# Six projections to the model width in a three-layer block: two matmuls of 256 columns become one of 512

## The chip, the core and the metric

The kernel runs on one core of one Trainium2 chip. The metric is device time in microseconds (us) of one launch. Before the change it was 1184.19, 1186.18 and 1185.54 us in three runs, median 1185.54 us.

## What is computed

The reference carries 256 tokens of width 1024 through three layers in float32: a Mamba-2 mixer with a convolutional feed-forward part ("ffn0"), differential attention with a second one ("ffn1"), and a layer with sparse attention beside a recurrent branch ("dsa") and a third one ("ffn2"). Each of the six parts ends in a projection back to the model width, whose result is added to `x`; the next part begins with a norm of that sum:

```python
for layer in range(DEPTH):
    ...
        mix = mamba2_mixer(x, ...)            # ... ends in  y @ out_w        2048 -> 1024
    ...
        mix = diff_attention(x, ...)          # ... ends in  o @ out_w        1024 -> 1024
    x = x + mix.astype(x.dtype)
    ff = conv_ffn(x, ...)                     # (silu(gate) * up) @ down_w    2816 -> 1024
    x = x + ff.astype(x.dtype)
```

The third layer has the same shape; its mixer ends in a 1024 to 1024 projection (`w_out_2`) whose result is scaled by a column of the modulation vector before it is added, as is that of its feed-forward part.

## The kernel before

**Two parts of every operand.** TensorE takes float32 operands here in a rounded form (`F32R`). To keep accuracy every operand is split into a high part (a rounded copy) and a low part (what is left). A product of W and x is three matmuls into the same PSUM tile: high by high, high by low, low by high. `mmB` (line 373) and `tileB_f` (line 780) write these three for each k tile of 128 rows, W stationary and x^T of 256 tokens moving, at lines 379 to 381 and 788 to 790.

**The weight stream.** Weights come from HBM in chunks through four `raw` buffers, SyncE issuing the DMA. `split` (line 242) makes of each piece (up to eight k tiles) `wh` on ScalarE (line 253) and `wl` on VectorE (line 257; at some steps on GpSimd, line 255). Both have five buffers, so pieces are split up to five ahead of TensorE, and a buffer comes free when TensorE has finished the piece that was in it.

**Steps.** The program is written as a list of steps, one for each piece. At the end of a step `step` (line 303) issues what was put off to it (the work behind a finished tile among that), then up to two splits, then a little background work. The engines' queues keep that order, apart from what the scheduler of the language puts forward.

**The projections.** `tileB` (line 421) makes one tile of 128 output channels: 22 k tiles for a feed-forward part (three pieces: 8, 8 and 6), 8 for `attn_out_w` and `w_out_2`. `tileB_f` does the same for the 16 k tiles of `ssm_out_w`. There are eight such tiles, m = 0 to 7, in each projection, and three PSUM buffers for them. When tile m is done, `add_x` (line 506) adds it to `x` on VectorE (line 509, or 511 with a scale), ScalarE squares the sum for the coming norm (line 440), and `mkraw` (line 393) makes unscaled high and low operands of the next part on ScalarE (line 396) and VectorE (line 397; two pairs where attention comes next). So the first tiles of the next part can begin before the norm is known; they need all eight tiles of `x`.

**The modulation.** From ffn0 to the end of ffn1 a vector product of 24 MB of weights runs beside all that, a little at each step (`ada`, line 546): a DMA of 256 KB into one of two buffers, and a multiply with a running sum on VectorE (line 553). During ffn0's and ffn1's projections and attention one such unit falls on each step.

Of the kernel before, what the change touches and what calls it, by code (L numbers as in the profile page):

```python
# [153 lines left out]
# columns of the constants  # L154
# [21 lines left out]
class Net:  # L176
# [3 lines left out]
    def __init__(self, ctx, tc, a, phases, dbg=None):  # L180
# [11 lines left out]
        self.whp = P("wh", self.NS)  # L192
        self.wlp = P("wl", self.NS)
# [35 lines left out]
    # -- weight stream --  # L229
# [12 lines left out]
    def split(self, pool=False):  # L242
# [8 lines left out]
        wh = self.whp.tile([128, 1024], F32R, name="wh")  # L251
        wl = self.wlp.tile([128, 1024], F32R, name="wl")
# [5 lines left out]
        self.spl[i] = (wh, wl)  # L258
# [13 lines left out]
    # -- ScalarE's function tables: one set at a time, changed where the program says --  # L272
# [75 lines left out]
    def pipe(self, n, stages, first=None):  # L348
        """item i runs its stage s at step i + s; of one step, `first` comes first, then later stages before earlier"""
# [14 lines left out]

    def ax(self):
        return self.axp.tile([128, 512], F32, name="ax")
# [5 lines left out]
    # -- W stationary, x^T moving: out [channels, tokens] --  # L372
    def mmB(self, out, src, kx, xh, xl, first, last, m=128):
        wh, wl = self.piece(src)
        n = len(kx)
        for a, k in enumerate(kx):
            h, l = wh[:, a * m:a * m + m], wl[:, a * m:a * m + m]
            nc = self.nc
            nc.tensor.matmul(out, h, xh[:, k, :], start=first and a == 0, stop=False)  # L379
            nc.tensor.matmul(out, h, xl[:, k, :], start=False, stop=False)  # L380
            nc.tensor.matmul(out, l, xh[:, k, :], start=False, stop=last and a == n - 1)  # L381

    def raw_tile(self):
        """unscaled operands [128, h/l, k, tokens and shift]"""
# [15 lines left out]
    def tileR(self, src, rw, shift, post, m=128, bg=1):  # L400
        """a tile from the operands before their scaling by token, which its result gets instead"""
# [3 lines left out]
        self.mmB(pt, src, range(8), rw[:, 0, :, 0:n], rw[:, 1, :, 0:n], True, True, m)  # L405
# [15 lines left out]
    def tileB(self, src, nk, xh, xl, post, m=128, bg=1, delay=1):  # L421
        pt = self.ps()[0:m, 0:T]
        k = 0
        while k < nk:
            n = min(8, nk - k)
            self.mmB(pt, src, range(k, k + n), xh, xl, k == 0, k + n == nk, m)
# [5 lines left out]
    # -- norms --  # L432
# [13 lines left out]
    def rstd_bc(self, parts, n, bcast=True):  # L446
        """1/sqrt(mean of squares + eps) of each token, on all partitions: [128, T] in PSUM"""
# [23 lines left out]
    def xn(self, i=0):  # L471
        h = self.xp.tile([128, 8, T], F32R, name=f"xh{i}")
        l = self.xp.tile([128, 8, T], F32R, name=f"xl{i}")
        return h, l

    def norm(self, g, shift=None):
        """the normed x, times the gains g(k), plus shift(k), in two parts"""
        nc = self.nc
        h, l = self.xn()
# [24 lines left out]
        return h, l  # L504
# [11 lines left out]
    def start_dsa(self):  # L516
        nc, P = self.nc, self.P
        # softplus(-lambda), times -8
# [12 lines left out]
    # -- c -> the six modulation vectors, a little at each step --  # L531
# [32 lines left out]
    # ---------------------------------------------------------------- Mamba-2  # L564
    def mamba(self, pool, nxt):
# [6 lines left out]
        xh, xl = self.norm(lambda k: P("ssm_ln_g", k))  # L572
# [74 lines left out]
        for t in range(8):  # L647
# [4 lines left out]
            else:  # L652
                self.tileB("ssm_in_w", 8, xh, xl, post)
        xs = self.xp.tile([128, 16, T], F32, name="rw")
        for t in range(16):
            self.tileB("ssm_in_w", 8, xh, xl, conv_post(t, xs[:, t, :]))
# [905 lines left out]
```

## Time and profile before

| What | Time |
|---|---|
| median of three runs | 1185.54 us |
| span of the profiled execution | 1186.9 us |
| TensorE busy in it | 1132.1 us |
| VectorE busy | 959.5 us |
| ScalarE busy | 712.5 us |
| GpSimd busy | 220.6 us |

The profiled execution is one launch; the span is from its first to its last instruction, and no other time of that launch is given. PE is TensorE's matmuls, PEld its weight loads, DVE VectorE, ACT ScalarE, POOL GpSimd, SP SyncE. A matmul's row gives a start and a duration; matmuls overlap, so what one costs in a stream is the distance between two starts, not the duration.

### The profile page before, as it was taken

Reading aid. Unit: us, or ns where it says so; the run is one execution under the profiler, and the core shown is the slowest. Engines: PE = TensorE matmul, PEld = TensorE weight load, DVE = VectorE, ACT = ScalarE, POOL = GpSimd, SP = SyncE. Lnnn points to the kernel's source line nnn. Section 1 sums busy time; section 2 is a strip of 40 time slices with the busy share of each in tenths; the row PEclk is TensorE's granted clock in tenths of the full one; section 3 lists DMA queues with packets and bytes.
Section 4 is the critical chain, followed back from the end, with each engine's and each line's share of the span. In section 5 each row is a group of like instructions: output and inputs, shape, how many; then the busy total and the mean of one; then the engine's idle time right before and its main releaser. Section 6 shows DMA issues by size and latency. Waiting matters only on the chain.

```text
span 1186.9 us, 23538 instructions
## 1 busy us (share of the span) xinstructions
PE 1132.1 (95%) x9174; PEld 1099.7 (93%) x9174; DVE 959.5 (81%) x1866; ACT 712.5 (60%) x1322; POOL 220.6 (19%) x180
## 2 busy tenths in 40 slices
PE   6899898999999989998899999899999999999997
PEld 5799897989999989988899999898999999999997
DVE  5897997789898888788899988768867888888752
ACT  6567665566666547876566664464587556666541
POOL 3203665242100114222320001100100023200010
PEclk9899999999999999999799999899999999999999
DMA  8455442647766886664366668844442653555440
GB/s 303 141 181 191 149 159 75 234 154 252 259 213 230 268 280 216 205 201 161 133 214 221 205 215 282 258 163 151 165 160 86 210 195 138 191 197 177 166 141 36
DMA packets 50190, 224.80 MB, mean 189 GB/s; under 512 B 5744, under 2 KB 10496, under 8 KB 31136
## 3 DMA queue, kind: packets, MB, share of 16 engines
q1 hardware_dynamic: 41616, 211.53, 52.1%
q10 hardware_dynamic: 7056, 7.46, 2.3%
q0 software_dynamic: 1408, 4.32, 1.2%
q8 instruction: 72, 1.18, 0.4%
q14 instruction: 38, 0.31, 0.1%
HBM read 222.11 MB, written 4.25 MB: 191 GB/s over the span
## 4 chain that ended last, share of the span: by engine, by line
PE 56%; DVE 16%; DMA 7%; issue 4%; ACT 3%; POOL 1%; POOLq 0%; ACTq 0%; DVEq 0%
PE mm L379 15%; PE mm L380 15%; PE mm L381 15%; DMA ada<-in_wada_dram 7%; DVE wl L257 4%; DVE ada L553 2%; DVE cv L817 2%; DVE ny L493 1%; PE mm L912 1%; PE mm L913 1%; PE mm L914 1%; PE mm L789 1%; ACT wh L253 1%; PE mm L788 1%; PE mm L790 1%
## 5 line engine op out<-in xcount | busy, mean ns | idle before, releaser
L253 ACT ACTIVATE wh<-raw 128x1024 fp32r<-128x1024 f32 (+2 forms) x360 | 369.6, 1030 | 267.4 <-PE mm L380 233.1
L257 DVE TENSOR_TENSOR wl<-raw,wh 128x1024 fp32r<-128x1024 f32 (+1 forms) x333 | 395.7, 1189 | 101.4 <-ACT wh L253 98.8
L379 PE MATMUL mm<-xh,wh 128*128 128x256 f32 x1624 | 466.9, 288 | 8.2 <-DVE cv L817 2.1
L380 PE MATMUL mm<-xl,wh 128*128 128x256 f32 x1624 | 461.4, 284 | 6.3 <-DVE xl L469 6.0
L381 PE MATMUL mm<-xh,wl 128*128 128x256 f32 x1624 | 459.8, 283 | 0.0
L379 PEld LDWEIGHTS mm<-xh,wh 128*128 128x128 f32 x1624 | 308.7, 190 | 17.4 <-issue 9.0
L380 PEld LDWEIGHTS mm<-xl,wh 128*128 128x128 f32 x1624 | 308.7, 190 | 8.4 <-DVE xl L469 8.0
L381 PEld LDWEIGHTS mm<-xh,wl 128*128 128x128 f32 x1624 | 308.7, 190 | 0.0
L444 POOL TENSOR_TENSOR sqacc<-sqacc,sq 128x256 f32<-128x256 f32 x42 | 49.3, 1174 | 563.2 <-ACT sq L440 561.7
L379 PE MATMUL mm<-hh,wh 128*128 128x256 f32 x528 | 147.4, 279 | 0.0
L381 PE MATMUL mm<-hh,wl 128*128 128x256 f32 x528 | 147.4, 279 | 0.0
L380 PE MATMUL mm<-hl,wh 128*128 128x256 f32 x528 | 147.4, 279 | 0.0
L817 DVE SCALAR_TENSOR_TENSOR cv<-mm,par,cv 128x255 f32<-128x255 f32 x240 | 114.3, 477 | 4.4 <-ACT cv L815 2.8
L379 PEld LDWEIGHTS mm<-hh,wh 128*128 128x128 f32 x528 | 99.2, 188 | 0.0
L380 PEld LDWEIGHTS mm<-hl,wh 128*128 128x128 f32 x528 | 99.2, 188 | 0.0
L381 PEld LDWEIGHTS mm<-hh,wl 128*128 128x128 f32 x528 | 99.2, 188 | 0.0
L255 POOL TENSOR_TENSOR wl<-raw,wh 128x1024 fp32r<-128x1024 f32 x27 | 71.9, 2668 | 132.3 <-ACT wh L253 132.2
L553 DVE SCALAR_TENSOR_TENSOR ada<-ada,silu_c 128x512 f32<-128x512 f32 x96 | 71.3, 744 | 21.8 <-DMA ada<-in_wada_dram 21.6
L815 ACT ACTIVATE cv<-mm,par 128x256 f32<-128x256 f32 x120 | 65.7, 548 | 0.3 <-PE mm L381 0.3
L379 PE MATMUL mm<-rw,wh 128*128 128x256 f32 (+2 forms) x168 | 51.1, 305 | 9.6 <-ACT wh L253 8.5
L380 PE MATMUL mm<-rw,wh 128*128 128x256 f32 (+2 forms) x168 | 51.9, 309 | 0.0
L440 ACT ACTIVATE sq<-x 128x256 f32<-128x256 f32 x49 | 20.0, 410 | 53.0 <-DVE x L509 34.2
(317 smaller groups left out, 1993.0 us busy)
## 6 DMA issues: line engine op xcount, KB each, us to landing
raw<-in_w_dram SPq DMA_DIRECT2D x148, 1024.0 KB, 4.9
ada<-in_wada_dram SPq DMA_DIRECT2D x96, 256.0 KB, 4.0
raw<-in_w_dram SPq DMA_DIRECT2D x23, 896.0 KB, 4.6
raw<-in_w_dram SPq DMA_DIRECT2D x6, 768.0 KB, 4.2
abc<-acs_scr ACTq DMA_DIRECT2D x16, 256.0 KB, 3.4
rel_bias_scr<-rel_bias_row POOLq DMA_DIRECT2D x8, 384.0 KB, 7.2
bias<-rel_bias_scr ACTq DMA_DIRECT2D x16, 128.0 KB, 4.4
x<-in_xT_dram SPq DMA_DIRECT2D x4, 256.0 KB, 4.1
```

The source lines that it names most:

```text
L253: nc.scalar.activation(wh[:, :n], src, AF.Copy)
L255: nc.gpsimd.tensor_tensor(wl[:, :n], src, wh[:, :n].bitcast(F32), op=ALU.subtract)
L257: self.pace = nc.vector.tensor_tensor(wl[:, :n], src, wh[:, :n].bitcast(F32), op=ALU.subtract)
L379: nc.tensor.matmul(out, h, xh[:, k, :], start=first and a == 0, stop=False)
L380: nc.tensor.matmul(out, h, xl[:, k, :], start=False, stop=False)
L381: nc.tensor.matmul(out, l, xh[:, k, :], start=False, stop=last and a == n - 1)
L440: nc.scalar.activation(s, self.x[:, k, :], AF.Square)
L444: nc.gpsimd.tensor_tensor(self.acc, self.acc, s, op=ALU.add)
L493: nc.vector.scalar_tensor_tensor(y, self.x[:, k, :], g(k), self.rsb, op0=ALU.mult, op1=ALU.mult)
L553: i = nc.vector.scalar_tensor_tensor(t, t, 1.0, self.sc[:, h * 512:h * 512 + 512], op0=ALU.mult, op1=ALU.mult, accum_out=self.part[:, h, m ...
L815: nc.scalar.activation(c, pt, AF.Identity, scale=w(2), bias=P(cb, ct))
L817: nc.vector.scalar_tensor_tensor(c[:, d:], pt[:, :T - d], w(2 - d), c[:, d:], op0=ALU.mult, op1=ALU.add)
```

## The change

In the six projections the two matmuls that share the weights' high part become one of 512 columns: it takes high and low part of x side by side, and leaves high by high in the first half of a PSUM bank and high by low in the second. Low by high still goes as 256 columns, onto the first half. On the way out `add_x` adds both halves to `x`, one after the other, so there are two VectorE instructions for each tile instead of one. The other matmuls stay as three. To let one access pattern reach both parts, pairs of tiles become one tile with a dimension of two (`wh`/`wl` to `ww`, `xh`/`xl` to `xx`, `hh`/`hl` to `hh`, and so on); sizes and numbers of buffers stay. Comments and docstrings go as well.

```diff
+    def ps_wide(self):
+        return self.ps().rearrange("p (a t) -> p a t", a=2)
...
-        wh = self.whp.tile([128, 1024], F32R, name="wh")
-        wl = self.wlp.tile([128, 1024], F32R, name="wl")
+        ww = self.wp.tile([128, 2, 1024], F32R, name="ww")
+        wh, wl = ww[:, 0], ww[:, 1]
...
+    def mm3(self, out, h, l, x, first, last):
+        nc = self.nc
+        if len(out.shape) == 3:
+            nc.tensor.matmul(out, h, x, start=first, stop=False)
+            nc.tensor.matmul(out[:, 0], l, x[:, 0], start=False, stop=last)
+            return
+        nc.tensor.matmul(out, h, x[:, 0], start=first, stop=False)
+        nc.tensor.matmul(out, h, x[:, 1], start=False, stop=False)
+        nc.tensor.matmul(out, l, x[:, 0], start=False, stop=last)
+
-    def mmB(self, out, src, kx, xh, xl, first, last, m=128):
-        wh, wl = self.piece(src)
+    def mmB(self, out, src, kx, xx, first, last, m=128):
+        ww = self.piece(src)
         n = len(kx)
         for a, k in enumerate(kx):
-            h, l = wh[:, a * m:a * m + m], wl[:, a * m:a * m + m]
-            nc = self.nc
-            nc.tensor.matmul(out, h, xh[:, k, :], start=first and a == 0, stop=False)
-            nc.tensor.matmul(out, h, xl[:, k, :], start=False, stop=False)
-            nc.tensor.matmul(out, l, xh[:, k, :], start=False, stop=last and a == n - 1)
+            c = slice(a * m, a * m + m)
+            self.mm3(out, ww[:, 0, c], ww[:, 1, c], xx[:, :, k, :], first and a == 0, last and a == n - 1)
...
-    def tileB(self, src, nk, xh, xl, post, m=128, bg=1, delay=1):
-        pt = self.ps()[0:m, 0:T]
+    def tileB(self, src, nk, xx, post, m=128, bg=1, delay=1, wide=False):
+        pt = self.ps_wide() if wide else self.ps()[0:m, 0:T]
...
     def add_x(self, m, pt, scale=None):
         nc = self.nc
-        if scale is None:
-            nc.vector.tensor_tensor(self.x[:, m, :], pt, self.x[:, m, :], op=ALU.add)
-        else:
-            nc.vector.scalar_tensor_tensor(self.x[:, m, :], pt, scale, self.x[:, m, :], op0=ALU.mult, op1=ALU.add)
+        for a in (1, 0):
+            if scale is None:
+                nc.vector.tensor_tensor(self.x[:, m, :], pt[:, a], self.x[:, m, :], op=ALU.add)
+            else:
+                nc.vector.scalar_tensor_tensor(self.x[:, m, :], pt[:, a], scale, self.x[:, m, :],
+                                               op0=ALU.mult, op1=ALU.add)
         self.square(m)
         self.mkraw(m)
...
         if pt is None:
-            pt = self.ps()[0:128, 0:T]
+            pt = self.ps_wide()
...
-            wh, wl = self.piece(src)
+            ww = self.piece(src)
             for a in range(n):
-                h, l = wh[:, a * 128:a * 128 + 128], wl[:, a * 128:a * 128 + 128]
-                nc.tensor.matmul(pt, h, fh(k + a), start=k + a == 0, stop=False)
-                nc.tensor.matmul(pt, h, fl(k + a), start=False, stop=False)
-                nc.tensor.matmul(pt, l, fh(k + a), start=False, stop=k + a == nk - 1)
+                c = slice(a * 128, a * 128 + 128)
+                self.mm3(pt, ww[:, 0, c], ww[:, 1, c], f(k + a), k + a == 0, k + a == nk - 1)
...
-        hh = pool.tile([128, NF, T], F32R, name="hh", bufs=1)
-        hl = pool.tile([128, NF, T], F32R, name="hl", bufs=1)
+        xx = self.norm(gs, shift=shift)
+        hh = pool.tile([128, 2, NF, T], F32R, name="hh", bufs=1)
...
-            self.tileB(down, NF, hh, hl, lambda pt, m=m: self.add_x(m, pt, scale and scale(m)))
+            self.tileB(down, NF, hh, lambda pt, m=m: self.add_x(m, pt, scale and scale(m)), wide=True)
...
-            self.tileB("attn_out_w", 8, oh, ol, lambda pt, m=m: self.add_x(m, pt))
+            self.tileB("attn_out_w", 8, oo, lambda pt, m=m: self.add_x(m, pt), wide=True)
...
-            self.tileB("w_out_2", 8, mh, ml, lambda pt, m=m: self.add_x(m, pt, self.mod[:, 16 + m:17 + m]))
+            self.tileB("w_out_2", 8, mx, lambda pt, m=m: self.add_x(m, pt, self.mod[:, 16 + m:17 + m]),
+                       wide=True)
```

## Rows read from the trace of the kernel before

**Rows 1.** The page: the span, and each engine's busy time, share and instructions.

```profile
span 1186.9 us, 23538 instructions
PE 1132.1 (95%) x9174; PEld 1099.7 (93%) x9174; DVE 959.5 (81%) x1866; ACT 712.5 (60%) x1322; POOL 220.6 (19%) x180
```

**Rows 2.** Windows, the six projections: stretch, length, busy times (instructions), clock, DMA.

```profile
206.00:234.70 28.70, 28.70 (x246) 28.70 (x245) 21.24 (x25) 15.60 (x24) 8.06 (x6) 1.00 0.64 210
368.00:429.70 61.70, 61.67 (x529) 61.47 (x527) 51.36 (x102) 32.82 (x48) 7.06 (x6) 1.00 0.79 268
541.00:561.60 20.60, 18.90 (x149) 18.29 (x148) 20.54 (x38) 13.15 (x22) 6.09 (x6) 0.97 0.66 215
697.60:759.30 61.70, 61.70 (x532) 61.70 (x530) 50.07 (x99) 31.54 (x43) 6.71 (x6) 1.00 0.81 265
957.60:981.00 23.40, 23.35 (x195) 23.14 (x194) 19.53 (x27) 13.98 (x25) 8.42 (x6) 1.00 0.58 208
1113.25:1174.90 61.65, 61.65 (x531) 61.65 (x530) 28.12 (x34) 23.26 (x31) 7.83 (x6) 1.00 0.30 103
```

**Rows 3.** Timeline, ends of tiles 0 and 7 in ffn0's projection, two engines.

```profile
375.49 0.28 PE L381 MATMUL mm<-hh,wl 128*128 128x256 f32 x1
376.44 0.42 DVE L509 TENSOR_TENSOR x<-mm,x 128x256 f32<-128x256 f32 x1
...
429.39 0.28 PE L381 MATMUL mm<-hh,wl 128*128 128x256 f32 x1
434.65 0.42 DVE L509 TENSOR_TENSOR x<-mm,x 128x256 f32<-128x256 f32 x1
435.63 0.61 PE L452 MATMUL ax<-onec,sq 128*128 128x1 f32 x4 [3.29 <-ACT sq L440]
```

**Rows 4.** Timeline, end of tile 7 in ffn1's and in ffn2's projection.

```profile
758.97 0.28 PE L381 MATMUL mm<-hh,wl 128*128 128x256 f32 x1
764.27 0.42 DVE L509 TENSOR_TENSOR x<-mm,x 128x256 f32<-128x256 f32 x1
...
1174.62 0.28 PE L381 MATMUL mm<-hh,wl 128*128 128x256 f32 x1
1174.94 0.48 DVE L511 SCALAR_TENSOR_TENSOR x<-mm,mod,x 128x256 f32<-128x256 f32 x1 [7.22 <-PE mm L381]
```

**Rows 5.** Timeline, the f32 matmuls of the recurrent gates among the others.

```profile
833.55 1.03 PE L1231 MATMUL ax<-xc,wg 128*128 128x256 f32 x4
834.22 0.47 PE L379 MATMUL mm<-xh,wh 128*128 128x256 f32 x1
834.53 0.28 PE L380 MATMUL mm<-xl,wh 128*128 128x256 f32 x1
```

**Rows 6.** Timeline, two matmuls at the start of ffn1.

```profile
562.06 0.41 PE L380 MATMUL mm<-rw,wh 128*128 128x256 f32 x1
562.28 0.41 PE L381 MATMUL mm<-rw,wl 128*128 128x256 f32 x1
```

**Rows 7.** Windows, two stretches behind a projection: columns as before.

```profile
437.50:440.90 3.40, 3.40 (x19) 3.40 (x18) 1.47 (x8) 1.05 (x2) 0.71 (x1) 0.51 0.96 313
560.50:567.20 6.70, 6.70 (x32) 6.70 (x33) 4.27 (x12) 1.24 (x3) 1.09 (x1) 0.50 0.81 267
```

**Rows 8.** Timeline, VectorE in attention's projection: the first three adds, and the last.

```profile
541.06 1.09 DVE L509 TENSOR_TENSOR x<-mm,x 128x256 f32<-128x256 f32 x3 [0.59 <-PE mm L381]
...
561.23 0.41 DVE L509 TENSOR_TENSOR x<-mm,x 128x256 f32<-128x256 f32 x1
```

**Rows 9.** Waits in ffn0's projection, then in ffn1's: total us, times, longest.

```profile
DVE ada L553 <- DMA ada<-in_wada_dram: 8.8, 7, 2.4
...
DVE ada L553 <- DMA ada<-in_wada_dram: 9.6, 7, 1.6
```

**Rows 10.** Timeline, VectorE early in ffn0's projection.

```profile
372.88 0.42 DVE L469 TENSOR_TENSOR hl<-cv,hh 128x256 fp32r<-128x256 f32 x1
```

More of the change, by code (lines that the diff above doesn't have):

```diff
@@ L404, in tileR @@
         pt = self.ps()[0:m, 0:n]
-        self.mmB(pt, src, range(8), rw[:, 0, :, 0:n], rw[:, 1, :, 0:n], True, True, m)
+        self.mmB(pt, src, range(8), rw[:, :, :, 0:n], True, True, m)
         if self.pre:
@@ L425, in tileB @@
             n = min(8, nk - k)
-            self.mmB(pt, src, range(k, k + n), xh, xl, k == 0, k + n == nk, m)
+            self.mmB(pt, src, range(k, k + n), xx, k == 0, k + n == nk, m)
             k += n
@@ L471, in xn @@
     def xn(self, i=0):
-        h = self.xp.tile([128, 8, T], F32R, name=f"xh{i}")
-        l = self.xp.tile([128, 8, T], F32R, name=f"xl{i}")
-        return h, l
+        return self.xp.tile([128, 2, 8, T], F32R, name=f"xx{i}")
     def norm(self, g, shift=None):
         nc = self.nc
-        h, l = self.xn()
+        xx = self.xn()
+        h, l = xx[:, 0], xx[:, 1]
         def start():
@@ L667, in yt @@
             if t < 8:
-                return yh01[:, t, :], yl01[:, t, :]
+                return y01[:, :, t, :]
             if not late:
-                late["h"], late["l"] = self.xn()
-            return late["h"][:, t - 8, :], late["l"][:, t - 8, :]
+                late["y"] = self.xn()
+            return late["y"][:, :, t - 8, :]
         def s0(t):
@@ L752, in s7 @@
             for i in range(t - 3, t + 1):
-                h, l = yt(i)
+                h, l = (yt(i)[:, a, :] for a in range(2))
                 nc.vector.scalar_tensor_tensor(xs[:, i, :], xs[:, i, :], hg[:, i:i + 1], bc, op0=ALU.mult, op1=ALU.mult)
@@ L762, in mamba @@
         for t in range(16):
-            self.tileB("ssm_in_w", 8, xh, xl, zpost(t))
-        yH = lambda k: yt(k)[0]
-        yL = lambda k: yt(k)[1]
-        pts = [self.tileB_f("ssm_out_w", 0, 8, 16, yH, yL) for m in range(AHEAD)]
+            self.tileB("ssm_in_w", 8, xx, zpost(t))
+        pts = [self.tileB_f("ssm_out_w", 0, 8, 16, yt) for m in range(AHEAD)]
         self.flush()
@@ L827, in comb @@
             nc.vector.tensor_tensor(u, g, u, op=ALU.mult)
-            self.later(1, lambda: self.split_act(u, hh[:, j, :], hl[:, j, :]))
+            self.later(1, lambda: self.split_act(u, hh[:, 0, j, :], hh[:, 1, j, :]))
         for j in range(NF):
@@ L834, in ffn @@
                 else:
-                    self.tileB(up, 8, xh, xl, conv(j, half))
+                    self.tileB(up, 8, xx, conv(j, half))
         self.flush()
@@ L900, in tok @@
         def tok(w, c):
-            xh, xl = xop[w]
+            xx = xop[w]
             src = "q_w" if w == "q" else "kv_w"
@@ L909, in tok @@
                 for k in range(8):
-                    wh, wl = ws[k // 4]
-                    cs = slice(k % 4 * 256, k % 4 * 256 + 256)
-                    nc.tensor.matmul(o, xh[:, k, s], wh[:, cs], start=k == 0, stop=False)
-                    nc.tensor.matmul(o, xh[:, k, s], wl[:, cs], start=False, stop=False)
-                    nc.tensor.matmul(o, xl[:, k, s], wh[:, cs], start=False, stop=k == 7)
+                    w2 = ws[k // 4][:, :, k % 4 * 256:k % 4 * 256 + 256]
+                    self.mm3(o, xx[:, 0, k, s], xx[:, 1, k, s], w2, k == 0, k == 7)
                 if tt == 1:
@@ L1060, in dsa @@
         self.since, self.part_of = 0, "dsa"
-        xh, xl = self.norm(lambda k: gm[:, k:k + 1], shift=lambda k: self.mod[:, k:k + 1])
+        xx = self.norm(lambda k: gm[:, k:k + 1], shift=lambda k: self.mod[:, k:k + 1])
         W = "w_in_2"
-        qT = tl("qT", [128, 4, T])
+        qq = tl("qq", [128, 2, 4, T])
+        qT, qi = qq[:, 0], qq[:, 1]
         kT = tl("kT", [128, T])
@@ L1197, in a4 @@
             if not OHL:
-                OHL.extend([tl("qT", [128, 4, T], d=F32R), tl("qi", [128, 4, T], d=F32R)])
-            oh, ol = OHL
+                OHL.append(tl("qq", [128, 2, 4, T], d=F32R))
+            oh, ol = OHL[0][:, 0], OHL[0][:, 1]
             p = self.ax()
@@ L1208, in dsa @@
         xc = tl("xc", [128, 8, T])
-        rr = tl("rr", [128, 8, T])
-        ii = tl("ii", [128, 8, T])
+        ri = tl("ri", [128, 2, 8, T])
+        rr, ii = ri[:, 0], ri[:, 1]
         gab = self.xp.tile([128, 16, T], F32, name="rw")
@@ L1308, in dsa @@
         self.out("gb", gb)
-        rh, rl = self.xn()
+        r2 = self.xn()
         for t in range(8):
-            self.split_act(yg[:, t, :], rh[:, t, :], rl[:, t, :])
-        mh = pool.tile([128, 8, T], F32R, name="rr", bufs=1)
-        ml = pool.tile([128, 8, T], F32R, name="ii", bufs=1)
+            self.split_act(yg[:, t, :], r2[:, 0, t, :], r2[:, 1, t, :])
+        mx = pool.tile([128, 2, 8, T], F32R, name="ri", bufs=1)
         for m in range(8):
             pa = self.ps()[:, 0:T]
-            self.mmB(pa, "w_o_attn_2", range(4), OHL[0], OHL[1], True, True)
+            self.mmB(pa, "w_o_attn_2", range(4), OHL[0], True, True)
             self.step()
             pr = self.ps()[:, 0:T]
-            self.mmB(pr, "w_o_rnn_2", range(8), rh, rl, True, True)
+            self.mmB(pr, "w_o_rnn_2", range(8), r2, True, True)
             def post(m=m, pa=pa, pr=pr):
@@ L1326, in post @@
                 nc.vector.scalar_tensor_tensor(t1, t2, 0.5, t1, op0=ALU.mult, op1=ALU.add)
-                self.later(1, lambda: self.split_act(t1, mh[:, m, :], ml[:, m, :]))
+                self.later(1, lambda: self.split_act(t1, mx[:, 0, m, :], mx[:, 1, m, :]))
             self.later(1, post)
```

49 lines of the change are left out of this document (22 added, 27 removed).

## The prediction

> **What bounds the kernel now.** I read the page first, then the busy times by stretch, then the timelines at the ends of the projections, then the waits inside them. The page says TensorE: busy 95% of the span, VectorE 81% [rows 1]. That is a mean over parts with different limits, and the change touches six stretches, so I took those by themselves [rows 2]. In all of them TensorE looks full. What tells them apart is VectorE: 28 of 62 us busy in ffn2's projection, 51 of 62 in ffn0's and 50 of 62 in ffn1's, and 20.54 of 20.60 in attention's, where it never rests.
>
> A busy share doesn't say who sets the end, so I looked at when the sum for a tile starts after the tile's last matmul. In ffn2 the last matmul of tile 7 ends at 1174.62 + 0.28 = 1174.90 and the add starts at 1174.94: VectorE was idle and waiting [rows 4]. In ffn0 the add of tile 0 comes 0.67 us after the matmul's end (375.77 to 376.44), that of tile 7 comes 4.98 us after it (429.67 to 434.65) [rows 3]. VectorE falls behind by some 0.6 us for each tile: its pace is (434.65 - 376.44) / 7 = 8.32 us a tile, TensorE's 61.70 / 8 = 7.71. ffn1 ends in the same way, 5.02 us behind (759.25 to 764.27) [rows 4]. The next part needs tile 7 of x, so after ffn0's projection TensorE soon stands idle, its last 3.29 us of waiting ended by the square of that sum [rows 3]. So of six projections three (mamba, dsa, ffn2) end when TensorE does, and three (ffn0, attention, ffn1) when VectorE does. The change takes work from the first engine and gives some to the second.
>
> **What a matmul costs.** In ffn2's projection 8 x 22 x 3 = 528 matmuls take 61.65 us, 116.8 ns each; in mamba's 28.70 / 246 = 116.7 [rows 2]. At the granted 2.4 GHz a column a clock would be 106.7 ns for 256. At half clock two starts are 0.22 apart, where a column a clock gives 0.213 [rows 6], so the extra 10 ns belongs to the full clock. No row shows a rounded matmul of 512 columns. The nearest stream of that length is the gates' full f32 matmul: between the first of four and the start of the second rounded matmul behind them lie 0.98 us [rows 5]; less one rounded matmul at 117, four take 863 ns, 216 each. That is twice 106.7 and 2.6 more, each with its own weight load. I take 216 for the 512 columns; the narrow matmul behind it stays at 116.7. A k tile then saves 2 x 116.7 - 216 = 17.4 ns. Bounds: 0, if the extra goes with the columns (512 at 233), and 20, if it goes wholly (213.3).
>
> The Trainium skill, "TensorE: Matmul & The Clock Gate", section Back-to-back issue gap, gives a warm matmul N/2.4 + 2.5 ns. The f32 row agrees with it; the 116.7 of the rounded ones stands 7.5 above its 109.2. By it a merged pair saves only 2.5 ns, and the saving below would be 0.6 us instead of 4.5; this is among the rivals.
>
> **What is removed, where TensorE sets the end.** Mamba: I count only the stretch in rows 2, 246 / 3 = 82 k tiles, 82 x 17.4 = 1.4 us. ffn2: 8 x 22 = 176 k tiles, 3.1 us. dsa: 64 k tiles would give 1.1, but VectorE there does 19.53 / 8 = 2.44 us a tile of 2.92; with 0.40 more it is at 2.84, and TensorE would be at 2.78. So VectorE takes the pace over at about 2.84, and 0.6 us are left.
>
> **What is added.** One more add for each of 48 tiles. Three adds in a row take 1.09 us and one 0.41 to 0.42 [rows 8, 3], so the next starts 0.335 us after the one before; that is the price in VectorE's queue. The scaled form takes 0.48 [rows 4], I put it at 0.40. The last second add of a projection is on the path everywhere: 0.34 for mamba, 0.40 each for dsa and ffn2. (The half with high by low is complete one matmul earlier; if its add may start then, 0.12 us of it comes back. I count none.) So mamba gains 1.1, dsa 0.2, ffn2 2.7: 4.0 us off.
>
> **Where VectorE sets the end.** There the faster TensorE gives little: it only waits longer. In attention's projection VectorE has no idle time in which to hide eight adds: 8 x 0.335 = 2.7 us later [rows 2, 8]. In ffn0 and ffn1 it does wait, 8.8 and 9.6 us, seven times each, for the DMA of a modulation unit [rows 9]. That DMA is issued when VectorE has done with the buffer, two units before; an add that falls in between eats of the wait, one that comes before the issue delays the DMA too, and the wait is as long as before. With three units and one add to a tile I take half as hidden: 1.3 of 2.7 us are left. While VectorE is still close behind TensorE, in the first tile, it gets its work earlier by up to 22 x 17.4 ns = 0.4; I take 0.3. So +1.0 each, bounds -0.4 and +2.7; for attention bounds 0 and +2.7. Together 4.7 us on.
>
> **Edits at nothing.** A weight buffer is now freed as one, so ScalarE may wait for the third matmul instead of the second, 0.12 us; the pieces split ahead cover it, and where they don't, VectorE is late by the same 0.12. The wide matmul needs the low part one matmul sooner: as much, and covered likewise. A PSUM buffer comes free 0.34 us later: with three buffers a tile two further on hides that while the lag is under two tiles, 15 us in the feed-forward parts. In attention two tiles are 5.8 us, and VectorE's pace is counted there anyway. TensorE's longer pause behind ffn0, attention and ffn1 may also cost clock: behind ffn0's projection 3.4 us run at 0.51, behind attention's 6.7 us at 0.50 [rows 7]. One more stretch of 3.4 us at half clock would cost 1.7; not in the sum, but in the upper end.
>
> **The sum.** -4.0 + 4.7 = +0.7 us on a span of 1186.9. That span is 1.4 us above the median of the runs; no other time of that execution is shown, and I carry the difference over to the median: 1185.5 + 0.7, rounded to 1186.3. A difference under 0.2% (2.4 us) can't be told from none here, so this is a forecast of no change that can be measured.
>
> **Rivals.**
> *VectorE's waits swallow the adds* (faster). For it: 8.8 and 9.6 us of waiting are far more than 2.7. Against: the lag grew to 5 us beside that waiting, so VectorE with its waits, not TensorE, had the pace. If all adds of ffn0 and ffn1 vanish and the 0.3 stays: -4.0 - 0.6 + 2.7 = -1.9; if TensorE's gain also arrives there (3.1 less 0.34 each): -4.0 + 2.7 - 5.5 = -6.8, 1178.7. Chance 0.27, mostly 1179 to 1183.5.
> *The adds pay the full price* (slower). Place: VectorE's queue in ffn0 and ffn1. Price 0.335 us an add; it decides if fewer than a quarter of them fall between a unit's DMA and the unit. Then 3 x 2.7 - 0.6 - 4.0 = +3.5, and with one more half-clock stretch +5.2: 1189 to 1190.7. Chance 0.15.
> *The 512 columns cost as much as two matmuls* (the change doesn't do what it says). For it: the rounded matmul's 10 ns may go with its columns. Against: the f32 row. Then the tails of 1.1 and 2.7 + 1.3 + 1.3 stay: +6.4, 1191.9. Chance 0.10. By the rule of the skill above it would be 0.6 us less, 1191.3.
> *Merged tiles make the wide read wait for the whole tile.* ffn0's last low part is written until 373.30 [rows 10], its projection runs from 368.0: 5.3 us for each of three, +16, 1202. Nothing in the trace of before has such a read; there the two parts are waited for by k tile. Chance 0.04.
>
> **Chances and range.** The forecast has 0.44, its own range 1183 to 1189, of it 0.03 below 1183.2 and 0.05 above 1187.9. Faster by over 0.2%: 0.27 + 0.03 = 0.30. Slower: 0.15 + 0.10 + 0.04 + 0.05 = 0.34. Within: 0.36. The range 1180.5 to 1191.5 leaves out the far end of the first rival (some 0.08), most of the last two and a little of the second (0.11).
>
> **What would show it.** In the profile after: starts of wide and narrow matmuls in ffn2's projection, 216 and 117 ns apart, and that projection in some 58.6 us; in attention's projection VectorE still without rest and about 2.7 us longer; in ffn0 and ffn1 a lag behind TensorE of some 9 us at tile 7, made of TensorE's 3.1 us lead and 1 us of adds, with the waits for modulation DMAs shorter by a little over 1 us each; no wait for a low part at a projection's first matmul. The prediction fails if the wide matmul is at 233, if the lag of VectorE is lower than now, or if the instructions in VectorE's queue come in another order than before.

## The result: 0.8% slower, and the profile after

| | before | after |
|---|---|---|
| median of four runs each | 1185.86 us | 1195.13 us |
| lowest and highest | 1184.19, 1187.67 | 1193.54, 1196.35 |
| span of the profiled execution | 1186.9 us | 1193.5 us |

The ratio is 1.0077, with a 95% interval of 1.0056 to 1.0097: some 9 us more, outside the predicted range. The span in the profiles grew by 6.6 us.

The page of the changed kernel, to be held beside [rows 1]:

```profile
span 1193.5 us, 21854 instructions
PE 1129.9 (95%) x8390; PEld 1064.0 (89%) x8390; DVE 978.4 (82%) x1914; ACT 718.4 (60%) x1322; POOL 209.5 (18%) x180
```

TensorE has 784 matmuls fewer and is busy 2.2 us less. VectorE has the 48 adds more and is busy 18.9 us more. Neither says where 9 us come from, so I go through the places that the prediction named.

**The wide matmul.** Timeline of TensorE in ffn2's projection:

```profile
1124.33 0.39 PE L380 MATMUL mm<-hh,ww 128*128 128x512 f32 x1
1124.56 0.28 PE L381 MATMUL mm<-hh,ww 128*128 128x256 f32 x1
1124.68 0.39 PE L380 MATMUL mm<-hh,ww 128*128 128x512 f32 x1
1124.90 0.28 PE L381 MATMUL mm<-hh,ww 128*128 128x256 f32 x1
```

From a wide start to the narrow one behind it: 0.23 us; back to the next wide one: 0.12. Over the three feed-forward projections, with 528 wide matmuls, the medians are 228 and 118 ns, so a k tile takes 346 ns where it took 350. A saving of 17.4 ns was predicted. The windows agree; this one is ffn2's projection, to be held beside the last line of [rows 2]:

```profile
1120.16:1181.34 61.18, 61.18 (x356) 54.25 (x355) 30.55 (x39) 23.83 (x30) 6.51 (x6) 1.00 0.31 109
```

61.2 us where it was 61.7; 58.6 were predicted.

**Attention's projection.** The window from its first add to the end of its last one:

```profile
550.10:574.00 23.90, 20.86 (x127) 17.86 (x126) 23.90 (x47) 13.66 (x22) 5.62 (x6) 1.00 0.58 193
```

VectorE (the third busy time) is busy in all 23.90 us; before, it was 20.6 us [rows 2]. The eight adds cost 3.3 us, not 2.7.

**The end of ffn0.** Timeline of TensorE and VectorE, tile 7 and what follows it, beside [rows 3]:

```profile
434.82 0.28 PE L381 MATMUL mm<-hh,ww 128*128 128x256 f32 x1
...
441.54 0.42 DVE L520 TENSOR_TENSOR x<-mm,x 128x256 f32<-128x256 f32 x1
441.87 1.21 DVE L256 TENSOR_TENSOR ww<-raw,ww 128x1024 fp32r<-128x1024 f32 x1
443.00 0.42 DVE L520 TENSOR_TENSOR x<-mm,x 128x256 f32<-128x256 f32 x1
...
443.98 1.02 PE L463 MATMUL ax<-onec,sq 128*128 128x1 f32 x4 [4.41 <-ACT sq L451]
```

The last matmul ends at 435.10, the second add starts at 443.00: a lag of 7.9 us where it was 4.98. The two adds of the tile are not neighbours: a split of weights stands between them and costs 1.13 us on the path. In the trace of the changed kernel another VectorE instruction stands between the two adds in 25 of the 48 tiles, in all eight of ffn0's. That is a first sign that VectorE's queue has a new order.

**The start of ffn0.** Nothing of the change was expected here. Timeline of all engines but the weight loads:

```profile
254.59 1.04 ACT L252 ACTIVATE ww<-raw 128x1024 fp32r<-128x1024 f32 x1
...
255.54 0.40 ACT L479 ACTIVATE xx<-ny 128x256 fp32r<-128x256 f32 x1
255.62 0.47 DVE L822 SCALAR_TENSOR_TENSOR cv<-ru,par,cv 128x255 f32<-128x255 f32 x1
...
255.71 2.59 POOL L254 TENSOR_TENSOR ww<-raw,ww 128x1024 fp32r<-128x1024 f32 x1 [5.34 <-ACT ww L252]
...
256.00 0.38 PE L383 MATMUL mm<-xx,ww 128*128 128x256 f32 x1
256.02 2.56 DVE L480 TENSOR_TENSOR xx<-ny,xx 128x256 fp32r<-128x256 f32 x1
...
258.64 0.58 PE L384 MATMUL mm<-xx,ww 128*128 128x256 f32 x1 [2.26 <-DVE xx L480]
```

TensorE waits from 256 us on for the low part of the eighth k tile of the normed x (line 480). ScalarE has put a copy of weights (line 252, 1.04 us) ahead of the high part that the low part is made from (line 479), VectorE a step of the convolution (line 822) ahead of the low part. So that starts at 256.02, just behind the start of a split on GpSimd, and needs 2.56 us instead of 0.41. In the kernel before, the seventh and the eighth low part come together, and the long VectorE instruction beside GpSimd's split is a later one:

```profile
250.90 3.85 POOL L255 TENSOR_TENSOR wl<-raw,wh 128x1024 fp32r<-128x1024 f32 x1 [4.47 <-ACT wh L253]
...
251.41 0.74 DVE L469 TENSOR_TENSOR xl<-ny,xh 128x256 fp32r<-128x256 f32 x2
...
252.42 2.62 DVE L817 SCALAR_TENSOR_TENSOR cv<-ru,par,cv 128x254 f32<-128x254 f32 x1
```

In the changed kernel TensorE then runs at half clock, as the window shows; the second line is the same place in the kernel before:

```profile
257.30:264.10 6.80, 5.46 (x25) 5.46 (x26) 6.52 (x11) 2.41 (x4) 1.00 (x1) 0.50 0.33 104
```

```profile
252.40:259.20 6.80, 6.77 (x56) 6.55 (x56) 6.80 (x11) 4.49 (x9) 2.35 (x1) 1.00 0.16 46
```

The profile of before has no half-clock stretch between 185 and 437 us.

### The profile page after: what moved, and what is told of

It is laid out like the page before. It is cut to its first block, busy times and chain, and to the rows that moved or that the text cites. A ratio compares the mean times of both kernels' runs of the same rounds, so it can differ in the third digit from the quotient of the medians.

```text
span 1193.5 us, 21854 instructions
## 1 busy us (share of the span) xinstructions
PE 1129.9 (95%) x8390; PEld 1064.0 (89%) x8390; DVE 978.4 (82%) x1914; ACT 718.4 (60%) x1322; POOL 209.5 (18%) x180
## 4 chain that ended last, share of the span: by engine, by line
PE 56%; DVE 12%; DMA 7%; issue 5%; ACT 3%; POOL 2%; ACTq 0%; POOLq 0%; DVEq 0%
PE mm L383 15%; PE mm L384 15%; PE mm L385 14%; DMA ada<-in_wada_dram 6%; PE mm L380 6%; PE mm L381 3%; DVE ww L256 3%; DVE ada L565 2%; DVE rw L408 1%; DVE ny L503 1%; ACT ww L252 1%; DVE cv L822 1%; DVE xx L480 1%; ACT L L287 1%; DVE x L520 1%
## 5 line engine op out<-in xcount | busy, mean ns | idle before, releaser
L384 PE MATMUL mm<-xx,ww 128*128 128x256 f32 x1624 | 463.1, 285 | 11.7 <-DVE xx L480 9.7
L383 PE MATMUL mm<-xx,ww 128*128 128x256 f32 x1624 | 467.0, 288 | 4.9 <-ACT BC L287 2.1
L385 PE MATMUL mm<-xx,ww 128*128 128x256 f32 x1624 | 461.0, 284 | 0.0
L256 DVE TENSOR_TENSOR ww<-raw,ww 128x1024 fp32r<-128x1024 f32 (+1 forms) x333 | 396.3, 1191 | 63.6 <-ACT ww L252 62.8
L252 ACT ACTIVATE ww<-raw 128x1024 fp32r<-128x1024 f32 (+2 forms) x360 | 368.0, 1026 | 105.5 <-PE mm L381 65.1
L384 PEld LDWEIGHTS mm<-xx,ww 128*128 128x128 f32 x1624 | 310.4, 191 | 14.2 <-DVE xx L480 11.7
L383 PEld LDWEIGHTS mm<-xx,ww 128*128 128x128 f32 x1624 | 309.8, 191 | 13.0 <-issue 3.1
L385 PEld LDWEIGHTS mm<-xx,ww 128*128 128x128 f32 x1624 | 310.1, 191 | 0.0
L380 PE MATMUL mm<-hh,ww 128*128 128x512 f32 x528 | 183.2, 390 | 0.0
L381 PE MATMUL mm<-hh,ww 128*128 128x256 f32 x528 | 148.9, 282 | 0.0
L380 PEld LDWEIGHTS mm<-hh,ww 128*128 128x128 f32 x528 | 99.1, 188 | 20.7
L381 PEld LDWEIGHTS mm<-hh,ww 128*128 128x128 f32 x528 | 99.8, 189 | 0.0
L254 POOL TENSOR_TENSOR ww<-raw,ww 128x1024 fp32r<-128x1024 f32 x27 | 67.6, 2505 | 135.2 <-ACT ww L252 131.9
L383 PE MATMUL mm<-rw,ww 128*128 128x256 f32 (+2 forms) x168 | 49.8, 300 | 9.4 <-ACT ww L252 8.7
L384 PE MATMUL mm<-rw,ww 128*128 128x256 f32 (+2 forms) x168 | 50.0, 299 | 0.0
L385 PE MATMUL mm<-rw,ww 128*128 128x256 f32 (+2 forms) x168 | 49.7, 296 | 0.0
L383 PEld LDWEIGHTS mm<-rw,ww 128*128 128x128 f32 (+1 forms) x168 | 33.0, 198 | 10.1 <-ACT ww L252 8.7
```

Source lines behind the costliest of these rows:

```text
L252: nc.scalar.activation(wh[:, :n], src, AF.Copy)
L254: nc.gpsimd.tensor_tensor(wl[:, :n], src, wh[:, :n].bitcast(F32), op=ALU.subtract)
L256: self.pace = nc.vector.tensor_tensor(wl[:, :n], src, wh[:, :n].bitcast(F32), op=ALU.subtract)
L380: nc.tensor.matmul(out, h, x, start=first, stop=False)
L381: nc.tensor.matmul(out[:, 0], l, x[:, 0], start=False, stop=last)
L383: nc.tensor.matmul(out, h, x[:, 0], start=first, stop=False)
```

## The experiments

The order in which the instructions start explains the last finding. The scheduler of the language decides the order in each queue, and it gives ScalarE and VectorE another one for the changed kernel. Put beside the trace of before, by operation, tile names and shapes and without the adds, at least 191 of 1,322 ScalarE and 281 of 1,818 VectorE instructions have moved. Most of that comes from one edit that the prediction put at nothing: the weights' high and low part in one buffer. With that edit and without the wide matmul (kernel 1 below) 181 and 251 have moved; with the two in buffers of their own and the rest of the tiles merged, none (kernel 2). *Old order* means below: ScalarE's and VectorE's instructions held in the order of kernel 2, which by these names is that of before, each second add right behind its first.

All runs in one table. Beside the ratio to before stand two means over a kernel's timed runs: *clock* is the span times (1 - mean granted clock), the time that would be lost if TensorE set the pace throughout; *rest* is the time less that. It is bookkeeping and no proof of a cause. The standard error of each is about 0.2 to 1.6 us. The first column is the number under which the text names a kernel.

| | kernel | median us | ratio, 95% interval | clock | rest |
|---|---|---|---|---|---|
| | before (107 runs) | 1186.2 | | 22.8 | 1163.0 |
| | after | 1195.1 | 1.0077 (1.0056 to 1.0097) | 27.4 | 1167.6 |
| 1 | merged, narrow, one add | 1195.1 | 1.0073 (1.0049 to 1.0097) | 29.2 | 1165.7 |
| 12 | the same once more | 1193.8 | 1.0071 (1.0046 to 1.0096) | 28.6 | 1164.4 |
| 2 | own weight buffers, narrow | 1186.4 | 0.9994 (0.9978 to 1.0010) | 23.2 | 1163.1 |
| 3 | own weight buffers, wide | 1193.6 | 1.0067 (1.0042 to 1.0091) | 25.9 | 1168.3 |
| 4 | after, no second add | 1191.4 | 1.0037 (1.0013 to 1.0062) | 27.5 | 1163.1 |
| 5 | merged, narrow, old order | 1188.9 | 1.0011 (0.9994 to 1.0027) | 23.1 | 1165.3 |
| 6 | own buffers, wide, old order | 1191.9 | 1.0037 (1.0019 to 1.0054) | 23.1 | 1168.2 |
| 7 | own buffers, two adds, no wide matmul, old order | 1190.9 | 1.0045 (1.0027 to 1.0063) | 24.1 | 1167.4 |
| 8 | wide in mamba, dsa, ffn2 only, old order | 1184.4 | 0.9991 (0.9972 to 1.0010) | 22.9 | 1161.7 |
| 9 | wide, 512 columns contiguous, old order | 1191.5 | 1.0060 (1.0041 to 1.0079) | 24.6 | 1167.1 |
| 10 | after, old order | 1191.7 | 1.0059 (1.0040 to 1.0079) | 23.2 | 1168.4 |
| 11 | wide in attention only, old order | 1188.5 | 1.0029 (1.0013 to 1.0045) | 21.4 | 1167.2 |
| 13 | merged, narrow, old order at ffn0's start | 1191.3 | 1.0041 (1.0018 to 1.0064) | 25.8 | 1164.7 |
| 14 | after, old order at ffn0's start | 1194.9 | 1.0082 (1.0054 to 1.0110) | 27.4 | 1167.1 |
| 15 | merged, narrow, old order in front | 1188.8 | 1.0025 (1.0007 to 1.0043) | 26.1 | 1162.1 |
| 16 | merged, narrow, old order behind | 1193.8 | 1.0066 (1.0042 to 1.0089) | 26.2 | 1167.3 |

**1. Merging alone.** Theory A: the new order. Theory B: the terms of the prediction with other sizes.

```diff
+WIDE = ()
...
-        pt = self.ps_wide() if wide else self.ps()[0:m, 0:T]
+        pt = self.ps_wide() if wide in WIDE else self.ps()[0:m, 0:T]
...
-        for a in (1, 0):
+        for p in (pt[:, 1], pt[:, 0]) if len(pt.shape) == 3 else (pt,):
```

> All tiles merged as in the change (ww, xx, hh, oo and so on), but every product as three matmuls of 256 columns and one add for each tile. Theory A (the merged weight buffer changes the order of the instructions in ScalarE's and VectorE's queues, and the milestone behind mamba's projection is 3.2 us late because of it): 3 to 5 us slower than before, about 1189 to 1191. Theory B (the 512-column matmul saves only some 4 ns a k tile, and the adds are paid in full; the merging is free): within 1.5 us of before.

Measured: 1195.1, as much as the whole loss without a wide matmul or a second add, and 4 us and more above what theory A expected. Theory B can't give that.

**2. Own weight buffers, narrow.**

```diff
-        ww = self.wp.tile([128, 2, 1024], F32R, name="ww")
-        wh, wl = ww[:, 0], ww[:, 1]
+        wh = self.whp.tile([128, 1024], F32R, name="wh")
+        wl = self.wlp.tile([128, 1024], F32R, name="wl")
```

> As the last one, but with the weights' high and low part in buffers of their own, as before the change; only the tiles of x and of the other moving operands are merged. Both theories: within 1.5 us of before, since the queues' order is nearly that of before. If it is 3 us slower, the merged moving operands and not the weight buffer are at fault.

Measured: 1186.4, as before. So of all the merging it is the weight buffer that costs.

**3. Own weight buffers, with the wide matmul and two adds** (edit of 2 in the changed kernel).

> The whole change (512 columns, two adds, merged moving operands), but the weights' high and low part in buffers of their own. Theory A: 3 to 5 us less than the changed kernel, about 1190 to 1192. Theory B: as the changed kernel, 1194 to 1196.

Measured: 1193.6. Neither theory: without the merged buffer most of the loss is still there. So the merged buffer isn't the only cost, and the costs don't simply add up to 9 us. The order isn't quite that of before here either: 32 ScalarE and 57 VectorE instructions have moved.

**4. No second add.**

```diff
-        for a in (1, 0):
+        for a in (0,):
```

> The changed kernel without the add of the second half: the product of the weights' high part and x's low part is left out of the result. Both theories give the price of 48 adds. If they are paid in full in attention, ffn0 and ffn1 (3 x 2.7 us) and once at the end of each of the others (1.1 us), 9 us less than the changed kernel, 1186; by the prediction's terms (2.7 + 1.3 + 1.3 + 1.1) 6.4 us less, 1189; if they are hidden, no less than 1194.

Measured: 1191.4, some 4 us less than the changed kernel and none of the three values expected; the ten runs reach from 1181.7 to 1197.0. The new order without the second adds is so still 4.4 us above before by the ratio. In its profile attention's projection, from first to last add, takes 20.54 us again, as before.

**5. Merging with the old order.** The instructions of ScalarE and VectorE are logged as the program is written, and each gets a dependency without a semaphore on the one that stands ahead of it in the order of kernel 2.

```diff
+        for a, b in zip(o[:-1], o[1:]):
+            tc.add_manual_dep(log[n][b].ins, log[n][a].ins.name,
+                              mybir.DependencyInfo(mybir.DependencyClass.NoSync, mybir.DependencyReason.DATA),
+                              reason="order")
```

> All tiles merged, three matmuls of 256 columns and one add, as in the merge-only run, but ScalarE's and VectorE's instructions are held in the order of the run with the weights' own buffers by dependencies that carry no semaphore. Theory A (the order of the two queues is what the merged weight buffer costs): back within 1.5 us of before, about 1186. Theory C (the joint release of the buffer is the cost: the copy by ScalarE waits for the third matmul and for VectorE's subtraction): stays at 1193 to 1196.

Measured: 1188.9, ratio 1.0011, that is 2.5 us above before by the medians and 1.3 by the ratio. Theory A holds in the main: of the 8 to 9 us the order alone makes some 6 or 7 (1.0073 and 1.0071 against 1.0011, the intervals apart); for the joint release of the buffer at most 3 us are left. In the table the difference between the two is in the clock column: 29 and 23. The place that the profile of after showed is where the two part; the window 256.5 to 263.3 of the merge-only kernel, then the same of this one:

```profile
256.50:263.30 6.80, 4.55 (x22) 4.53 (x22) 6.80 (x11) 2.40 (x4) 1.94 (x1) 0.50 0.20 42
```

```profile
256.50:263.30 6.80, 6.78 (x57) 6.57 (x56) 6.80 (x10) 4.63 (x10) 1.89 (x1) 1.00 0.22 73
```

22 matmuls at a clock of 0.50 against 57 at 1.00. The two profiled launches lie at opposite ends, 1192.2 us the fastest of four and 1193.1 the slowest of twelve, so they show a place where the kernels differ and not what it costs in the median. (Instructions of kernels with a held order all carry the line of the helper that logs them, so tiles tell them apart.)

**6 to 8. The adds and the wide matmul in the old order**, own weight buffers: wide in all six; two adds, but high by high and high by low as two matmuls of 256; wide in mamba, dsa and ffn2 alone.

```diff
-            nc.tensor.matmul(out, h, x, start=first, stop=False)
+            nc.tensor.matmul(out[:, 0], h, x[:, 0], start=first, stop=False)      # 7 only
+            nc.tensor.matmul(out[:, 1], h, x[:, 1], start=False, stop=last, skip_group_check=True)
```

> 512 columns and two adds in all six projections, weights in buffers of their own, ScalarE's and VectorE's instructions held in the order of the kernel without the wide matmul, each second add right behind its first. Theory A (order also made most of the 7.5 us of the run with own weight buffers): what is left are the terms of the prediction with the measured 4 ns a k tile: -1.3 for the matmuls, +1.1 for the ends of mamba, dsa and ffn2, +2.7 for attention, 0 to 2.7 each for ffn0 and ffn1: 1188.5 to 1192. Theory D (the adds and the matmul's size make all of it): 1193 to 1195.

> As the last one, but high by high and high by low as two matmuls of 256 columns into the two halves: the adds without the 512 columns. Both theories: 1 to 1.5 us slower than the last one, since a k tile costs 350 ns instead of 346. If it is faster than the last one, the wide matmul costs by something else than its length.

> 512 columns and two adds only in the projections of mamba, dsa and ffn2, the others narrow with one add; own weight buffers and order held as in the last two. By the terms: -1.3 for the matmuls and +1.1 for the last adds: within 1.5 us of before, 1186. The difference to the run with all six is then the price of the adds in attention, ffn0 and ffn1.

Measured: 1191.9, 1190.9 and 1184.4. The adds cost with or without the 512 columns; between 6 and 7 no difference can be told. With the change in the three projections that TensorE sets, the kernel can't be told from before; between 6 and 8 lie 0.46% or 5.5 us for attention, ffn0 and ffn1 (7.5 by the medians). Timeline of VectorE in 6, the first three tiles of attention's projection, six adds:

```profile
541.69 2.46 DVE L192 TENSOR_TENSOR x<-mm,x 128x256 f32<-128x256 f32 x6 [0.71 <-PE mm L192]
```

Six take 2.46 us where three took 1.09 [rows 8]: each second add is (2.46 - 1.09) / 3 = 0.457 us, not 0.335. It needs the sum that the first one writes. The trace of before has such a price on view in dsa: two neighbours of which the second needs what the first writes start 0.46 us apart (0.455 in the median of six such pairs), where steps of that size that don't need each other start 0.33 apart:

```profile
936.41 0.42 DVE L1325 SCALAR_TENSOR_TENSOR mt<-rw,mm 128x256 f32<-128x256 f32 x1 [0.26 <-PE mm L381]
936.87 0.42 DVE L1326 SCALAR_TENSOR_TENSOR mt<-mt,mt 128x256 f32<-128x256 f32 x1
```

The two scaled adds of a tile start 0.51 us apart (median of dsa and ffn2 in kernel 10), where 0.40 was put in.

**9. The 512 columns as one run of addresses** (kernel 6 otherwise; the other moving operands of the projections likewise).

```diff
-        hh = pool.tile([128, 2, NF, T], F32R, name="hh", bufs=1)
+        hh = pool.tile([128, NF, 2, T], F32R, name="hh", bufs=1).rearrange("p k a t -> p a k t")
```

> As the run with 512 columns in all six projections and the old order, but the high and the low part of each k tile lie beside each other in SBUF, so that the 512 columns are one run of addresses instead of two of 256. If the 228 ns between the start of a wide matmul and the narrow one behind it come from the two runs: 216 ns, ffn2's projection 2 us shorter, 2 to 4 us less than that run. If they go with the columns: still 228, and the same time within 1.5 us.

Timeline of TensorE in ffn2's projection:

```profile
1120.66 0.39 PE L192 MATMUL mm<-hh,wh 128*128 128x512 f32 x1
1120.89 0.28 PE L192 MATMUL mm<-hh,wl 128*128 128x256 f32 x1
1121.01 0.39 PE L192 MATMUL mm<-hh,wh 128*128 128x512 f32 x1
1121.24 0.28 PE L192 MATMUL mm<-hh,wl 128*128 128x256 f32 x1
```

Still 0.23 us, 228 ns in the median, and 1191.5 us where kernel 6 had 1191.9. The cost goes with the columns.

**10. The whole change in the old order.**

> The whole change as it is, weights merged, but ScalarE's and VectorE's instructions held in the order of the kernel before, each second add right behind its first. If order and adds are prices that add up, the order's part goes and the adds' stays: 1190 to 1192.5, as the run with own weight buffers, wide matmul and old order. If the adds are hidden behind the waits that the new order makes: no less than 1194.

Timeline of GpSimd and VectorE at the place of the pause in the changed kernel:

```profile
253.43 3.85 POOL L191 TENSOR_TENSOR ww<-raw,ww 128x1024 fp32r<-128x1024 f32 x1 [4.47 <-ACT ww L191]
...
253.94 0.74 DVE L191 TENSOR_TENSOR xx<-ny,xx 128x256 fp32r<-128x256 f32 x2
254.61 0.41 DVE L191 TENSOR_TENSOR cv<-cv,cv 128x256 f32<-128x256 f32 x1
254.94 2.61 DVE L191 SCALAR_TENSOR_TENSOR cv<-ru,par,cv 128x254 f32<-128x254 f32 x1
```

The seventh and the eighth low part come together, and the long instruction beside GpSimd is again a step of the convolution, for which TensorE doesn't wait.

Measured: 1191.7, 5.9 us above before by the medians and 7.0 by the ratio (4.7 to 9.4). So some 2 to 3 us of the 9 go with the order (medians 1195.1 and 1191.7; the intervals of the ratios overlap), and the clock column falls from 27.4 to 23.2. The rest column stays, 1167.6 and 1168.4. The second adds are neighbours of the first here, so their place in the queue is part of the difference; it wasn't held by itself.

**11. Wide in attention alone.**

> 512 columns and two adds in attention's projection alone; own weight buffers, old order. If VectorE's lack of rest there is what makes the adds cost: attention's projection 24.0 us instead of 20.6 from first to last add and most of the 5 us between the runs with six and with three wide projections, so 1189 to 1191. If ffn0 and ffn1 carry it: 1187 to 1188.

Measured: 1188.5, 3.4 us by the ratio (1.5 to 5.3), a little under the expected time. Its projection takes 24.15 us from first to last add. Attention carries most of the 5.5 us; what is left for ffn0 and ffn1, about 2, is within the uncertainty of these runs.

**12. Merging once more** (kernel 1).

> The merge-only kernel once more, with more rounds beside its partner with the old order. Theory A: 1193 to 1196, as the first time, 6 us or more above the same kernel in the old order. If it comes out under 1190, the first reading was chance.

Measured: 1193.8, above kernel 5 by 4.9 us in the medians and by 7.1 in the ratios, each to its own runs of before; 6 or more were expected. The reading stands, its size to some 2 us.

**13 and 14. The old order only at ffn0's start**, 33 VectorE and 24 ScalarE instructions, in kernel 1 and in the changed kernel.

```diff
+ORDER = {"scalar": old[296:320], "vector": old[362:395]}       # 13; written out, the kernel has the lists packed
```

> The merge-only kernel with the old order of ScalarE and VectorE only at the start of ffn0, 33 and 24 instructions long; all other places keep the new order. Theory F (the place is the loss): the pause of 2.6 us before the eighth k tile's low part falls under 1 us, the 6.8 us at half clock behind it go, 4 to 5 us less than the merge-only kernel: 1188.5 to 1190.5. Theory G (the loss is spread over many places): within 1.5 us of it, 1192.5 to 1196.

> The whole change with the old order of ScalarE and VectorE only at the start of ffn0. Theory F: 1190 to 1191.5, as the whole change with the old order everywhere. Theory G: 1193.5 to 1196, as the whole change.

Measured: 1191.3 and 1194.9. In both profiles the pause at 256 us is gone and no half-clock stretch follows it. In kernel 1 that is worth about 3 us, between what theory F and theory G said, and the intervals of the ratios overlap; in the whole change nothing that can be seen. There its profile reaches ffn0's last add 4.8 us earlier (438.6 for 443.4) and is behind by 0.3 us at the end: attention, ffn1 and dsa each take longer. The half-clock stretches behind ffn0's and attention's projections are 10.2 us each in it, where they are 6.8 in the changed kernel's profile, so as much of it stands there more as went at ffn0's start. Theory F fails for the whole change.

**15 and 16. The old order in front of that place and with it, or behind it**, in kernel 1.

```diff
+ORDER = {"scalar": old[:320], "vector": old[:395]}       # 15; written out as well
+ORDER = {"scalar": old[320:], "vector": old[395:]}       # 16
```

> The merge-only kernel with the old order of ScalarE and VectorE from the start up to ffn0's first tiles (the first 260 us) and the new order behind it. Theory F (the loss is made in mamba and at ffn0's start): within 1.5 us of the fully held one, 1186.5 to 1189. Theory G (spread): half of the way, 1190 to 1192. Theory H (the loss is behind): 1193 to 1195.

> The reverse: the new order up to ffn0's first tiles, the old one behind it. Theory F: 1192 to 1195. Theory G: 1190 to 1192. Theory H: 1186.5 to 1189.

Measured: 1188.8 and 1193.8. As theory F has it, the order of the first 260 us, mamba's part and ffn0's start, carries most of the price; that behind it costs nothing that can be told. Only 43 of the 181 moved ScalarE and 58 of the 251 moved VectorE instructions stand in front, by the trace of 16. The two columns don't say how the price is paid: kernel 16 has it as much in the rest (1167.3) as in the clock (26.2), and kernel 15, near kernel 5 in time, has a clock column of 26.1.

## Why the prediction was wrong, point by point

**Edits at nothing: the step that failed.** "A weight buffer is now freed as one", with 0.12 us covered by the pieces ahead. The release itself is small (kernel 5: at most 3 us, and zero is within its interval). But one buffer instead of two changed what the scheduler put where, and kernels 1, 5 and 12 show that this alone costs 6 to 7 us. How much of it is TensorE's clock is open: by the columns most of it in kernels 1 and 12, less than half in kernel 16. The prediction named a new order in VectorE's queue as a sign of failure and gave it no price. The part of it seen in the rows is the low part at 256 us, which another split pushed back; which of the other places in mamba carry the rest stays open. This step isn't the only one: with the old order the whole change still costs 5.9 to 7.0 us (kernel 10) where +0.7 was predicted, so a term of the sum failed too, the saving of the wide matmul: 1.3 us instead of 5.1. With what the adds cost more, 0.3 us at the ends of mamba, dsa and ffn2 and 0.8 in the other three, that makes 0.7 + 3.8 + 0.3 + 0.8 = 5.6 us.

**What a matmul costs.** 216 ns were taken for 512 columns from the gates' f32 matmul [rows 5]. Each of its four matmuls has 256 columns; that one takes twice as long as a rounded one of 256 says nothing about 512 rounded columns. The measured 228 lies near the other end, 233, so the rival with 512 at the price of two had the matmul almost right. The k tile saves 4 ns instead of 17.4, so 82 + 64 + 176 k tiles of mamba, dsa and ffn2 give 1.3 us and not the 1.4 + 0.6 + 3.1 = 5.1 of the prediction. By the formula that the Trainium skill, "TensorE: Matmul & The Clock Gate", section Back-to-back issue gap, gives for a warm matmul by itself, 512 columns would take 215.8 ns, an estimate. The rounded matmuls here don't agree, 228 ns in a stream, in two runs of addresses or in one.

**What is added.** -4.0 us were predicted for the three projections that TensorE sets; kernel 8 shows -0.09% (-0.28 to +0.10), no change that can be told. With the measured sizes the sum of these three is near nothing: 1.3 us saved, and second adds at the ends of 0.46, 0.51 and 0.51 us instead of 0.34, 0.40 and 0.40.

**Where VectorE sets the end.** The sign and the place were right. Attention: +2.7 predicted; its projection grew by 3.3 to 3.6 us in every kernel with two adds, since a dependent add costs 0.457 us. All three projections: +4.7 predicted, 5.5 measured between kernels 6 and 8. The claim that half of the adds in ffn0 and ffn1 hide in waits for the modulation's DMA was not settled: their lengths scatter by 2 us and more from profile to profile (first to last add of ffn0: 57.1 to 61.5 us over the profiles with one add, 57.7 to 61.4 over those with two). The means of these profiles, eleven and seven, differ by 0.8 us in ffn0 and 1.1 in ffn1, with standard errors of some 0.6, near the +1.0 each that was predicted. The waits don't bear out how: they should have been shorter by a little over 1 us each, but they are longer by 0.7 us in ffn0 and shorter by 2.9 in ffn1. From the projection's start to its last add, for ffn0 before and after, then for ffn1 before and after:

```profile
DVE ada L553 <- DMA ada<-in_wada_dram: 8.8, 7, 2.4
DVE ada L565 <- DMA ada<-in_wada_dram: 9.5, 7, 2.8
...
DVE ada L553 <- DMA ada<-in_wada_dram: 11.4, 8, 1.7
DVE ada L565 <- DMA ada<-in_wada_dram: 8.5, 8, 2.1
```

The lag of 9 us at tile 7 was predicted for the wrong reason: 7.9 came, of which TensorE's lead is 0.7 (176 x 4 ns) and 1.13 the split between the last two adds.

**The rivals.** "The 512 columns cost as much as two matmuls" (1191.9) comes out at what the change costs in the old order, 1191.7. "The adds pay the full price" (1189 to 1190.7) lies a little under it, since it kept the matmul's gain. "Merged tiles make the wide read wait for the whole tile" didn't happen: no such wait stands at the start of a feed-forward projection. No rival had the order, and with it comes 1195.

**The sum, mended.** Where TensorE sets the end, about +0.2 (adds +1.5, matmuls -1.3); in the other three projections +5.5; the order +2 to +3 on top of that: 7.7 to 8.7 of the measured 9 (6.6 to 11.5). Order alone, kernels 1 and 12 over kernel 5, is 0.6%, and the change in the old order, kernel 10, is 0.59%; together they would give 1.2%, and 0.77% (0.56 to 0.97) is measured. So the two overlap; where, is not shown.

## What to carry to other kernels

Where a scheduler orders the queues, a change of buffers can be a change of order (one buffer for the two parts of the weights was, one tile for those of x was not): compare the queues before pricing anything else, and when a regression can't be found in the edited lines, hold the old order and time again. A merged matmul saves only what is measured between its own kind of starts; a row of another data type is no substitute. An extra step on a saturated engine that needs the result of the one ahead of it costs its dependent price, not that of a stream of independent ones.

What was tried gives no version that beats the kernel before; the one with the change in mamba, dsa and ffn2 alone is at 0.9991 (0.9972 to 1.0010).

## What the runs showed of the hardware

- Rounded matmuls of 512 columns start 228 ns ahead of the next at full clock, 0.445 ns a column; 256 columns take 116 to 118. One run of addresses or two makes no difference.
- A VectorE add that needs the result of the one before it costs 0.457 us, an independent one 0.335 (128 x 256, f32, kernel 6 and [rows 8]); another dependent pair in the kernel before has 0.455.
- A 128 x 256 subtraction of VectorE with two inputs in SBUF took 2.56 us beside a GpSimd one of 2.59 us that began 0.31 us earlier, and 0.41 alone. Which VectorE instruction is hit is a matter of order: with the old one it is a step of the convolution that TensorE doesn't wait for. The Trainium skill, "SBUF — State Buffer", section SBUF: two separate sides, says that the two engines share a pair of ports which one of them holds for a whole instruction; these rows agree, the VectorE instruction ending 0.28 us behind GpSimd's (a GpSimd span is rough). In the old order three VectorE steps take their usual time inside a GpSimd span of 3.85 us and only the next one is long, so such a span seems to hold waiting of GpSimd's own.
- A pause of TensorE of 2.6 us between two starts at ffn0's start had a stretch of 6.8 us at a granted clock of 0.50 (1.2 GHz) beginning in it, in the profiles of all five kernels with the new order there (after, 1, 4, 12 and 16); with the old order neither stood there, nor in kernel 3. At that clock the stretch costs up to 6.8 x 0.5 = 3.4 us of work, an estimate, less what falls in the pause itself.
